# Weighing the attention's exponentials on ScalarE, and spreading a layer's modulations over nine groups of projections

## The chip, the cores and the metric

The kernel runs on one core of a Trainium2 chip. The metric is device time in microseconds (us), from one launch; the times here are medians of a few runs. The engines are TensorE (PE in the rows, with PEld for its weight loads), VectorE (DVE), ScalarE (ACT), GpSimd (POOL) and SyncE (SP), whose queue issues most loads by DMA.

## The reference, cut to what matters

An encoder trunk of two layers for 256 tokens of width 1024: layer 0 mixes tokens with RWKV-7, layer 1 with dilated attention, and behind each comes a mixture of experts (MoE). Every sub-layer is modulated: `shift`, `scale` and `gate` are rows of `silu(c) @ ada_w[layer] + ada_b[layer]`, six of width 1024 in each layer. The change lies in the attention, where each of 8 heads has three groups of keys, and the three results are merged by their softmax denominators:

```python
def _dilated_group(q, k, v, slopes, window, dilation):
    ...
    scores = jnp.where(valid, scores + alibi[None, None], NEG_INF)
    m = jnp.max(scores, axis=-1, keepdims=True)
    e = jnp.exp(scores - m)
    den = jnp.sum(e, axis=-1, keepdims=True)
    o = jnp.einsum('brhnqk,brhnkd->brhnqd', e, vblk) / den
    lse = (m + jnp.log(den))[..., 0]
    ...

def dilated_attention_mix(h, w_qkv, w_o):
    ...
    o = jnp.stack(outs)
    alpha = jax.nn.softmax(jnp.stack(lses), axis=0)
    merged = jnp.sum(alpha[..., None] * o, axis=0).reshape(bsz, s, d)
    return jnp.einsum('bsd,de->bse', merged.astype(h.dtype), w_o)
```

## The kernel before, in words

The attention is `heads()`. It takes the 8 heads as four pairs (`hp` 0 to 3). For each pair and each of three groups of keys (`g`), `project(hp, g)` makes q, k and v: a weight tile of 1 MB comes by SP's queue into `wring`, `weights()` splits it into two fp16 halves of which the sum is the weight (`wh` by ACT in L469 or L465/L466, `wl` by DVE in L473 or, for the second half of q's and v's weights, by POOL in L467), and PE multiplies the pieces in 48 matmuls of 128x256 (`qkv`, L271). The result is split in the same way (`qh` by ACT, `ql` by DVE).

`scores()` makes the scores of a group (`sc` on PE), adds the distance and takes the row maximum on DVE (L1800 to L1805), and ACT takes the exponential in place with the row sum (L1809). `merge()` is a chain of tiny DVE steps (L1816 to L1828) with one exponential on ACT (L1820); it gives `wg`, one factor per query, group and head. `values()` then multiplies each block of exponentials by its column of `wg` in place, in L1837: per head two blocks of 128x256 and four of 128x128. PE transposes the weighed blocks (`eT`, L275), ACT and DVE split the transposes (`eh`, `el`), PE multiplies them with v (`av`), and ACT and DVE split the result into `mh` and `ml`.

Beside this run two other jobs. The modulations of layer 1 are 32 *eighths*, four modulations by eight slices of 128 rows of `w_ada`. `ada()` takes an eighth from a ring of two buffers (`aring`, loaded by SP's queue), and DVE adds it, times `silu`, to `acc` in two pieces of 512 columns (L374 for the first eighth of a modulation, L376 for the others). After the last eighth of one, PE sums `acc` over the partitions (`ada` matmuls). For the gates (modulations 2 and 5) ACT's queue first loads the bias (L442) and DVE adds the two sums to it (L448). `ADA_PARTS` says how many eighths are handled behind each group of projections. The second job is the output weights: POOL multiplies them by gate 2 in L590, in four pieces per tile.

The program is written in the order of the loops in L1866 to L1894, and a scheduler puts each engine's instructions into a fixed order when the kernel is built. So the `merge` and `values` of a pair run while PE does the first projections of the next pair, and the engines wait for one another at run time. Pair 3 has no next pair; its cover is the output projection (`wo`). The MoE of layer 1 follows, whose 96 weight tiles of 1 MB come through the same SP queue.

Of the kernel before, what the change touches and what calls it, by code (L numbers as in the profile page):

```python
# [14 lines left out]
AF = mybir.ActivationFunctionType  # L15
ALU = mybir.AluOpType
# [16 lines left out]
RANK = dict(X=0, C=1, R=2, F=3, D=4, G=5, S=6, H=6, W=7, A=2.5)  # L33
OFFSET = dict(X=0, C=-6, R=-4, F=-2, D=-2, G=-1, S=0, H=0, W=0, A=8)

ADA_PARTS, PACE = (4, 4, 4, 4, 4, 4, 4, 4, 0), 4.0


C_TMG, C_CMG, C_ADAB, C_C, C_FG = 0, 16, 32, 128, 136
# [195 lines left out]
def trunk(ctx, tc, names, aps, out, stages=("rwkv", "moe0", "attn", "moe1"), dbg=None, ring=2):  # L235
# [12 lines left out]
    def bank(name="ps", tag="ps"):  # L248
        return psum[-1][tag].tile([128, 512], F32, name=name, tag=tag)
# [23 lines left out]
    def tr(o, i):  # L273
        pe_work[0] += 0.25
        return on_pe(nc.tensor.transpose(o, i, IDENT[0:i.shape[0], 0:i.shape[0]]))  # L275
# [27 lines left out]
    V, A, P = nc.vector, nc.scalar, nc.gpsimd  # L303
# [157 lines left out]
    def split(hi, lo, src, by, eng=None):  # L461

        if eng:
            if by != 1.0:
                A.activation(out=src, in_=src, func=AF.Copy, scale=by)  # L465
            A.activation(out=hi, in_=src, func=AF.Copy)  # L466
            eng.tensor_tensor(out=lo, in0=src, in1=hi, op=ALU.subtract)  # L467
            return
        A.activation(out=hi, in_=src, func=AF.Copy, scale=by)  # L469
        if by == 1.0:  # L470
            V.tensor_tensor(out=lo, in0=src, in1=hi, op=ALU.subtract)
            return
        V.scalar_tensor_tensor(out=lo, in0=src, scalar=by, in1=hi, op0=ALU.mult, op1=ALU.subtract)  # L473
# [1238 lines left out]
    def triple(o, lhs, rhs, start, stop):  # L1712

        for n, (a, b) in enumerate(((0, 0), (1, 0), (0, 1))):
            mm(o, lhs[a], rhs[b], start=start and n == 0, stop=stop and n == 2, skip_group_check=True)
# [6 lines left out]
    def heads(outer, mh, ml, before, c4):  # L1722
# [43 lines left out]
        scale = 128 ** -0.5  # L1766
# [64 lines left out]
        def values(hp, a, qkv, E, wg):  # L1831

            eh, el = (pool.tile([128, 8, 128], F16, name=n) for n in ("eh", "el"))
            for g in range(3):
                for t in range(NTT):
                    e = E[g][:, a, t * KW[g]:(t + 1) * KW[g]]
                    V.tensor_scalar(out=e, in0=e, scalar1=wg[:, t, g, a:a + 1], scalar2=None, op0=ALU.mult)  # L1837
            blocks = [E[0][:, a, t * 256 + kt * 128:t * 256 + kt * 128 + 128] for kt in range(2) for t in range(NTT)]
            blocks += [E[g][:, a, t * 128:(t + 1) * 128] for g in (1, 2) for t in range(NTT)]
            for n in range(2):  # L1840
                ps = bank(name="eT", tag="eT")
                for b in range(4):
                    tr(ps[:, b * 128:(b + 1) * 128], blocks[4 * n + b])
                split(*(v[:, 4 * n:4 * n + 4].rearrange("p b n -> p (b n)") for v in (eh, el)), ps, WSC)
            po = bank(name="av", tag="eT")
            vcol = slice(a * 128, a * 128 + 128)

            def av(o, v, c, start, stop):
                triple(o, [t[:, v[1], vcol] for t in qkv[v[0]][2]],
                       [t[:, c].rearrange("p b n -> p (b n)") for t in (eh, el)], start, stop)  # L1850

            for kt in range(2):
                av(po[:, 0:S], (0, kt), slice(2 * kt, 2 * kt + 2), kt == 0, False)
            for g in (1, 2):
                for t in range(NTT):
                    av(po[:, t * 128:(t + 1) * 128], (g, t), slice(2 + 2 * g + t, 3 + 2 * g + t), False,
                       g == 2 and t == 1)
            split(*(v[:, 2 * hp + a].rearrange("p (l r) -> p r l", r=NTT) for v in (mh, ml)),
                  po[:, 0:S].rearrange("p (r l) -> p r l", r=NTT), 1.0 / WSC)
# [6 lines left out]
        for hp in range(4):  # L1866
# [20 lines left out]
            wg = merge(st)  # L1887
# [211 lines left out]
```

## Time and profile before

| | us |
|---|---|
| median of 3 runs | 1186.47 |
| lowest, highest | 1184.41, 1190.94 |
| profiled execution, its own time | 1182.29 |
| its span, first to last instruction | 1180.5 |

| engine | busy us | share of the span |
|---|---|---|
| PE | 1040.8 | 88% |
| PEld | 682.5 | 58% |
| DVE | 616.8 | 52% |
| ACT | 432.4 | 37% |
| POOL | 148.7 | 13% |

The profile is of one execution. Busy time of PE is from modelled ends of pipelined matmuls. The granted clock is the share of TensorE's full clock that the chip allowed; over the span it was 0.943. A row of a timeline gives start, length, engine, line and operation; what stands in brackets at its end is the idle time of the engine before it and the instruction that ended that. "x8" means eight instructions in a row, merged into one row.

### The profile page before, as it was taken

What the parts mean: (1) busy time and instruction counts of PE and PEld (TensorE: products, weight loads), DVE (VectorE), ACT (ScalarE), POOL (GpSimd) and SP (SyncE); (2) the same over time, 40 slices, a digit from 0 to 9 for tenths busy, and PEclk for the clock granted to TensorE, in tenths of its full rate; (3) what the DMA queues carried; (4) which work ended last, traced back from release to release, by engine and by line L of the source; (5) the groups of instructions that cost most, each with busy time, mean ns of one, the idle gap of its engine ahead of it and who ended that gap; (6) DMA issues with size and microseconds to landing.
All of it is one profiled execution on the core that took longest, in us unless ns stands there. A gap on an engine that the chain in (4) does not pass through costs nothing.

```text
span 1180.5 us, 25023 instructions
## 1 busy us (share of the span) xinstructions
PE 1040.8 (88%) x10580; PEld 682.5 (58%) x10580; DVE 616.8 (52%) x1458; ACT 432.4 (37%) x915; POOL 148.7 (13%) x110
## 2 busy tenths in 40 slices
PE   7789999998978998978987799899979999789886
PEld 2576677766757655435442388777858754354422
DVE  4864678578485446213111467988885762131112
ACT  2634455455445342101000377555544621010012
POOL 1100010010012600000000112123373000000000
PEclk9879899899988899989999999998989999899999
DMA  9561524325233676998999987877744589989995
GB/s 366 207 220 60 180 67 159 114 89 167 73 130 132 263 286 250 400 414 361 422 421 421 420 346 262 310 268 284 255 173 150 212 352 395 416 362 421 420 421 238
DMA packets 53197, 322.01 MB, mean 273 GB/s; under 512 B 5922, under 2 KB 6562, under 8 KB 21458
## 3 DMA queue, kind: packets, MB, share of 16 engines
q1 hardware_dynamic: 51986, 315.88, 68.7%
q0 software_dynamic: 800, 3.36, 0.8%
q8 instruction: 87, 1.43, 0.5%
q10 hardware_dynamic: 288, 1.05, 0.3%
q14 instruction: 36, 0.29, 0.1%
HBM read 319.22 MB, written 1.05 MB: 271 GB/s over the span
## 4 chain that ended last, share of the span: by engine, by line
PE 23%; DMA 21%; DVE 8%; ACT 2%; issue 1%; ACTq 0%; SPq 0%; DVEq 0%
DMA wring<-in_w_moe_dram 21%; PE qkv L271 11%; PE gu L271 3%; DVE acc L376 2%; PE xT L271 1%; PE wo L271 1%; DVE wl L473 1%; PE acc L271 1%; PE dn L271 1%; PE av L271 1%; PE eT L275 1%; PE sc L271 1%; ACT sq L491 0%; DVE ql L473 0%; DVE E L1837 0%
## 5 line engine op out<-in xcount | busy, mean ns | idle before, releaser
L271 PE MATMUL gu<-wring,xT 128*32 128x512 f32 x1024 | 132.5, 617 | 18.0 <-DMA wring<-in_w_moe_dram 10.8
L376 DVE SCALAR_TENSOR_TENSOR acc<-aring,silu,acc 128x512 f32<-128x512 f32 x140 | 116.1, 859 | 13.2 <-DMA aring<-in_w_ada_dram 13.0
L467 POOL TENSOR_TENSOR wl<-wring,wh 128x1024 f16<-128x1024 f32 x24 | 57.7, 2406 | 409.4 <-DMA wring<-in_w_qkv_dram 248.3
L271 PE MATMUL qkv<-hl,wh 128*128 128x256 f16 x384 | 106.2, 277 | 2.0 <-DVE hl L1762 2.0
L271 PE MATMUL qkv<-hh,wh 128*128 128x256 f16 x384 | 106.3, 277 | 1.6 <-ACT hh L1761 1.6
L271 PE MATMUL qkv<-hh,wl 128*128 128x256 f16 x384 | 106.1, 277 | 1.2 <-DVE wl L473 1.1
L271 PEld LDWEIGHTS gu<-wring,xT 128*32 128x32 f32 x1024 | 31.3, 112 | 101.5 <-issue 78.1
L271 PEld LDWEIGHTS <-wh 128*128 128x128 f16 x768 | 76.3, 100 | 13.1 <-issue 3.6
L271 PE MATMUL dn<-wring,hidT 128*32 128x256 f32 x1024 | 66.2, 407 | 18.1 <-ACT hidT L1564 18.1
L473 DVE SCALAR_TENSOR_TENSOR wl<-wring,wh 128x1024 f16<-128x1024 f32 x56 | 70.6, 1266 | 16.6 <-ACT wh L469 16.6
L271 PE MATMUL acc<-y,back 128*128 128x512 f32 (+1 forms) x144 | 64.2, 568 | 10.3 <-DVE y L1591 8.1
L469 ACT ACTIVATE wh<-wring 128x1024 f16<-128x1024 f32 x56 | 58.6, 1050 | 35.6 <-PE qkv L271 30.9
L271 PEld LDWEIGHTS xT<-oh,x 128*128 128x128 f32 x512 | 59.0, 192 | 21.1 <-issue 9.2
L1366 DVE SCALAR_TENSOR_TENSOR sg<-sg,gu 128x256 f32<-128x256 f32 x16 | 6.7, 420 | 119.3 <-ACT sg L1365 119.3
L271 PE MATMUL xT<-oh,x 128*128 128x128 f32 x512 | 63.5, 280 | 2.5 <-DVE oh L1475 2.5
L1591 DVE TENSOR_TENSOR y<-dn,ga 128x512 f32<-128x512 f32 x28 | 19.4, 692 | 87.1 <-PE dn L271 55.5
L1365 ACT ACTIVATE sg<-gu 128x256 f32<-128x256 f32 x16 | 6.1, 384 | 147.3 <-PE gu L271 147.3
L271 PEld LDWEIGHTS dn<-wring,hidT 128*32 128x32 f32 x1024 | 32.3, 116 | 48.0 <-ACT hidT L1564 22.0
L271 PE MATMUL qkv<-wl,hh 128*128 128x256 f16 x192 | 54.0, 281 | 0.0
L271 PE MATMUL qkv<-wh,hh 128*128 128x256 f16 x192 | 53.9, 281 | 0.0
L271 PE MATMUL qkv<-wh,hl 128*128 128x256 f16 x192 | 53.9, 281 | 0.0
L1507 ACT ACTIVATE back<-bT 128x256 f32<-128x256 f32 x16 | 6.2, 386 | 129.7 <-PE acc L271 129.7
(355 smaller groups left out, 2096.5 us busy)
## 6 DMA issues: line engine op xcount, KB each, us to landing
wring<-in_w_moe_dram SPq DMA_DIRECT2D x192, 1024.0 KB, 19.8
aring<-in_w_ada_dram SPq DMA_DIRECT2D x96, 512.0 KB, 4.7
wring<-in_w_qkv_dram SPq DMA_DIRECT2D x36, 1024.0 KB, 8.7
wring<-in_w_kr_dram SPq DMA_DIRECT2D x8, 1024.0 KB, 5.4
wring<-in_w_vl_dram SPq DMA_DIRECT2D x8, 640.0 KB, 4.6
wring<-in_w_rwo_dram SPq DMA_DIRECT2D x4, 1024.0 KB, 8.2
wring<-in_w_ato_dram SPq DMA_DIRECT2D x4, 1024.0 KB, 6.9
x<-in_x_dram POOLq DMA_DIRECT2D x2, 512.0 KB, 7.7
```

The costliest lines, as they stand in the source:

```text
L271: return on_pe(nc.tensor.matmul(out=o, lhsT=lhsT, rhs=rhs, start=start, stop=stop, **kw))
L275: return on_pe(nc.tensor.transpose(o, i, IDENT[0:i.shape[0], 0:i.shape[0]]))
L376: V.scalar_tensor_tensor(out=acc[:, s], in0=w[:, s], scalar=silu[:, k:k + 1], in1=acc[:, s], op0=ALU.mult, op1=ALU.add)
L467: eng.tensor_tensor(out=lo, in0=src, in1=hi, op=ALU.subtract)
L469: A.activation(out=hi, in_=src, func=AF.Copy, scale=by)
L473: V.scalar_tensor_tensor(out=lo, in0=src, scalar=by, in1=hi, op0=ALU.mult, op1=ALU.subtract)
L1365: A.activation(out=o, in_=ps[:, 0:256], func=AF.Tanh, scale=0.5)
L1366: V.scalar_tensor_tensor(out=o, in0=o, scalar=1.0, in1=ps[:, 0:256], op0=ALU.add, op1=ALU.mult)
L1507: A.activation(out=back, in_=ps[:, 0:S], func=AF.Copy)
L1591: V.tensor_tensor(out=y, in0=py[c], in1=gates[i, 5][:, c * 512:(c + 1) * 512], op=ALU.mult)
```

## The change

The weighing of L1837 goes from VectorE to ScalarE, as a copy with a scale per partition: 48 instructions in all, six for each of eight heads. And the 32 eighths of layer 1's modulations are dealt out to nine groups of projections (five times four, then four times three) in place of eight groups of four. The numbers of `ADA_PARTS` go by `3 * hp + g`, so they cover pairs 0 to 2.

```diff
-ADA_PARTS, PACE = (4, 4, 4, 4, 4, 4, 4, 4, 0), 4.0
+ADA_PARTS, PACE = (4, 4, 4, 4, 4, 3, 3, 3, 3), 4.0
...
             for g in range(3):
                 for t in range(NTT):
                     e = E[g][:, a, t * KW[g]:(t + 1) * KW[g]]
-                    V.tensor_scalar(out=e, in0=e, scalar1=wg[:, t, g, a:a + 1], scalar2=None, op0=ALU.mult)
+                    A.activation(out=e, in_=e, func=AF.Copy, scale=wg[:, t, g, a:a + 1])
```

Three places show how the fixed order moves. The first is ACT at pair 0, from the split of q of the next pair on. `E0` to `E2` are the exponentials of the three groups, `eT` the transposes in PSUM, `eh` their fp16 heads, `wh` heads of projection weights. Before:

```order
L469 ACTIVATE qh01_9673<-qkv_9672 128x512
L469 ACTIVATE wh_9816<-wring_8799 128x1024
L469 ACTIVATE eh_9512<-eT_9520 128x512
L469 ACTIVATE eh_9512<-eT_9527 128x512
L469 ACTIVATE mh_8688<-av_9534 128x2x128
L469 ACTIVATE eh_9555<-eT_9563 128x512
L466 ACTIVATE wh_9820<-wring_8799 128x1024
L469 ACTIVATE eh_9555<-eT_9570 128x512
```

With the change:

```order
L469 ACTIVATE qh01_9673<-qkv_9672 128x512
L469 ACTIVATE wh_9816<-wring_8799 128x1024
L1837 ACTIVATE E0_9184<-E0_9184,wg_9497 128x256 x2
L1837 ACTIVATE E1_9425<-E1_9425,wg_9497 128x128 x2
L1837 ACTIVATE E2_9468<-E2_9468,wg_9497 128x128 x2
L469 ACTIVATE eh_9512<-eT_9520 128x512
L469 ACTIVATE eh_9512<-eT_9527 128x512
L1837 ACTIVATE E0_9184<-E0_9184,wg_9497 128x256 x2
L1837 ACTIVATE E1_9425<-E1_9425,wg_9497 128x128 x2
L1837 ACTIVATE E2_9468<-E2_9468,wg_9497 128x128 x2
L466 ACTIVATE wh_9820<-wring_8799 128x1024
```

The six weighings of the first head stand ahead of its splits, and the six of the second head behind them.

The second place is DVE in the merge of pair 1. `den`, `mm` and `wg` are the merge's small tiles, `acc` the accumulator of a modulation. Before:

```order
L376 SCALAR_TENSOR_TENSOR acc_10033<-aring_10274,silu_103,acc_10033 128x512 x2
L1822 TENSOR_TENSOR den_10325<-wg_10320,st0_10006 128x4
L1824 TENSOR_TENSOR mm_10317<-wg_10320,st1_10241 128x4
L1825 TENSOR_TENSOR den_10325<-den_10325,mm_10317 128x4
L374 TENSOR_SCALAR acc_10614<-aring_10278,silu_103 128x512
L1824 TENSOR_TENSOR mm_10317<-wg_10320,st2_10292 128x4
L374 TENSOR_SCALAR acc_10614<-aring_10278,silu_103 128x512
L1825 TENSOR_TENSOR den_10325<-den_10325,mm_10317 128x4
L367 TENSOR_TENSOR modc_107<-ada_10282,cols_66 128x8
L1826 RECIPROCAL den_10325<-den_10325 128x4
```

With the change:

```order
L1822 TENSOR_TENSOR den_10312<-wg_10307,st0_10006 128x4
L1824 TENSOR_TENSOR mm_10304<-wg_10307,st1_10241 128x4
L376 SCALAR_TENSOR_TENSOR acc_10033<-aring_10274,silu_103,acc_10033 128x512
L1825 TENSOR_TENSOR den_10312<-den_10312,mm_10304 128x4
L376 SCALAR_TENSOR_TENSOR acc_10033<-aring_10274,silu_103,acc_10033 128x512
L1824 TENSOR_TENSOR mm_10304<-wg_10307,st2_10279 128x4
L1825 TENSOR_TENSOR den_10312<-den_10312,mm_10304 128x4
L1826 RECIPROCAL den_10312<-den_10312 128x4
L1828 TENSOR_TENSOR wg_10307<-wg_10307,den_10312 128x2x2 x3
L473 SCALAR_TENSOR_TENSOR ql01_10484<-qkv_10482,qh01_10483 128x512
```

The two L374, which begin the next modulation, and the split `ql01` now stand behind the merge. On PE the first transposes of pair 1 follow 10 matmuls of the projection then running where 17 stood, and the matmuls of the finished modulation stand behind them. In pair 0 the first transposes follow 18 where 9 stood.

The third place is the merge of pair 2, on DVE and on POOL. `ga5` is gate 5 of the layer, `wl` the fp16 rests of projection weights. DVE before:

```order
L1819 TENSOR_TENSOR wg_11115<-st2_11087,mm_11112 128x2x2
L473 SCALAR_TENSOR_TENSOR wl_11293<-wring_10176,wh_11292 128x1024
L1822 TENSOR_TENSOR den_11120<-wg_11115,st0_10822 128x4
L1824 TENSOR_TENSOR mm_11112<-wg_11115,st1_11061 128x4
L1825 TENSOR_TENSOR den_11120<-den_11120,mm_11112 128x4
L1824 TENSOR_TENSOR mm_11112<-wg_11115,st2_11087 128x4
L1825 TENSOR_TENSOR den_11120<-den_11120,mm_11112 128x4
L473 SCALAR_TENSOR_TENSOR ql00_11235<-qkv_11233,qh00_11234 128x512
L1826 RECIPROCAL den_11120<-den_11120 128x4
```

DVE with the change:

```order
L1819 TENSOR_TENSOR wg_11115<-st2_11087,mm_11112 128x2x2
L448 TENSOR_TENSOR ga5_11078<-ga5_11078,ada_11080 128x512
L1822 TENSOR_TENSOR den_11120<-wg_11115,st0_10813 128x4
L1824 TENSOR_TENSOR mm_11112<-wg_11115,st1_11043 128x4
L1825 TENSOR_TENSOR den_11120<-den_11120,mm_11112 128x4
L473 SCALAR_TENSOR_TENSOR wl_11293<-wring_10176,wh_11292 128x1024
L448 TENSOR_TENSOR ga5_11078<-ga5_11078,ada_11083 128x512
L1824 TENSOR_TENSOR mm_11112<-wg_11115,st2_11087 128x4
L473 SCALAR_TENSOR_TENSOR ql00_11235<-qkv_11233,qh00_11234 128x512
L1825 TENSOR_TENSOR den_11120<-den_11120,mm_11112 128x4
L473 SCALAR_TENSOR_TENSOR wl_11352<-wring_10408,wh_11351 128x1024
L1826 RECIPROCAL den_11120<-den_11120 128x4
```

POOL before:

```order
L467 TENSOR_TENSOR wl_11229<-wring_10113,wh_11228 128x1024
L590 TENSOR_TENSOR wring_11220<-wring_11220,ga2_9226 128x512 x4
L590 TENSOR_TENSOR wring_11222<-wring_11222,ga2_9226 128x512 x4
L467 TENSOR_TENSOR wl_11356<-wring_10421,wh_11355 128x1024
L467 TENSOR_TENSOR wl_11420<-wring_10485,wh_11419 128x1024
```

POOL with the change:

```order
L467 TENSOR_TENSOR wl_11229<-wring_10113,wh_11228 128x1024
L467 TENSOR_TENSOR wl_11356<-wring_10408,wh_11355 128x1024
L590 TENSOR_TENSOR wring_11220<-wring_11220,ga2_9226 128x512 x4
L590 TENSOR_TENSOR wring_11222<-wring_11222,ga2_9226 128x512 x4
L467 TENSOR_TENSOR wl_11420<-wring_10472,wh_11419 128x1024
```

The two additions of gate 5 come into the merge of pair 2, and one split more; on POOL a split moves ahead of eight gatings. ACT issues the load of gate 5's bias behind the exponentials of `E1` of pair 2, where it issued it behind those of `E0`. PE does 20 more matmuls of projections, and the second one of gate 5, ahead of the first transposes of this pair. In pair 3, ACT splits two halves of output weights ahead of its first weighing, and four more output matmuls stand ahead of the first transposes, two more behind them.

## Rows read from the trace of the kernel before

**Rows 1.** The page, the chain that ended last: share of the span by engine.
```profile
PE 23%; DMA 21%; DVE 8%; ACT 2%; issue 1%; ACTq 0%; SPq 0%; DVEq 0%
```

**Rows 2.** The chain in order of time, its tail: start us, us, what.
```profile
1137.12 19.80 DMA wring<-in_w_moe_dram
```

**Rows 3.** Waits of SP's DMA queue, 860–960: us in total, times, longest.
```profile
SPq L153 <- DVE wl L473: 50.8, 10, 10.4
```

**Rows 4.** Stretches: us, busy PE, PEld, DVE, ACT, POOL, then PEclk, DMA, GB/s.
```profile
752.00:782.00 30.00, 25.63 (x208) 21.40 (x207) 24.44 (x32) 13.35 (x18) 6.58 (x3) 0.89 0.83 304
...
808.00:828.00 20.00, 17.57 (x136) 14.64 (x137) 16.61 (x38) 8.61 (x15) 5.80 (x2) 0.83 0.62 233
...
873.00:890.00 17.00, 9.23 (x77) 7.82 (x75) 15.05 (x32) 7.10 (x17) 10.24 (x6) 0.80 0.19 63
...
890.00:930.00 40.00, 40.00 (x377) 35.81 (x376) 20.32 (x25) 21.42 (x31) 8.51 (x4) 1.00 0.53 185
```

**Rows 5.** PE's waits in 678–950 us: us in total, times, longest.
```profile
PE eT L275 <- DVE E L1837: 11.2, 4, 7.8
PE ada L271 <- DVE acc L376: 4.4, 3, 2.6
```

**Rows 6.** One 2 us window of PE: us, busy, clock, DMA share, GB/s.
```profile
756.00:758.00 2.00, 2.00 (x12) 0.50 0.91 352
```

**Rows 7.** Groups by form, 678–950 us: busy us, mean ns, idle before.
```profile
L1837 DVE TENSOR_SCALAR E<-E,wg 128x128 f32<-128x128 f32 x32 | 8.9, 336 | 0.0
...
L1837 DVE TENSOR_SCALAR E<-E,wg 128x256 f32<-128x256 f32 x16 | 4.9, 345 | 0.0
...
L1809 ACT ACTIVATE E<-E,neg 128x256 f32<-128x256 f32 x16 | 7.9, 497 | 0.9 <-DVE neg L1805 0.9
```

**Rows 8.** Timeline of ACT, pairs 2 and 3: start, us, instruction.
```profile
869.42 0.38 ACT L1809 ACTIVATE E<-E,neg 128x128 f32<-128x128 f32 x1
869.71 0.19 ACT L1809 ACTIVATION_READ_ACCUMULATOR E<-E,neg 128x1 f32 x1
...
936.15 1.99 ACT L469 ACTIVATE wh<-wring 128x1024 f16<-128x1024 f32 x2
```

**Rows 9.** Timeline of DVE, pair 0 and the quarter behind it.
```profile
746.23 1.91 DVE L1837 TENSOR_SCALAR E<-E,wg 128x256 f32<-128x256 f32 x8
...
749.32 2.73 DVE L376 SCALAR_TENSOR_TENSOR acc<-aring,silu,acc 128x512 f32<-128x512 f32 x4
...
752.30 2.74 DVE L1837 TENSOR_SCALAR E<-E,wg 128x128 f32<-128x128 f32 x4
...
773.88 3.27 DVE L376 SCALAR_TENSOR_TENSOR acc<-aring,silu,acc 128x512 f32<-128x512 f32 x2
```

**Rows 10.** The page, the modulations' loads: KB each, us to landing.
```profile
aring<-in_w_ada_dram SPq DMA_DIRECT2D x96, 512.0 KB, 4.7
```

**Rows 11.** Timeline of DVE, then of PE, pair 1.
```profile
814.25 0.48 DVE L374 TENSOR_SCALAR acc<-aring,silu 128x512 f32<-128x512 f32 x1 [1.33 <-PE ada L271]
...
816.58 2.31 DVE L1837 TENSOR_SCALAR E<-E,wg 128x256 f32<-128x256 f32 x10
...
812.64 0.51 PE L271 MATMUL ada<-cst,acc 128*128 128x1 f32 x3 [0.91 <-DVE acc L376]
```

**Rows 12.** Timeline of PE, pair 2, group 1.
```profile
846.47 1.13 PE L271 MATMUL ada<-acc,cst 128*128 128x512 f32 x2 [0.85 <-DVE acc L376]
```

**Rows 13.** Timelines of DVE, PE and POOL, the merge of pair 2.
```profile
872.98 2.35 DVE L1819 TENSOR_TENSOR wg<-st,mm 128x4 f32<-128x4 f32 x3
...
881.59 0.47 PE L275 MATMUL eT<-cst,E 128*128 128x128 f32 x1 [7.77 <-DVE E L1837]
...
868.14 11.89 POOL L590 TENSOR_TENSOR wring<-wring,ga 128x512 f32<-128x512 f32 x8
```

**Rows 14.** Timeline of DVE, the merge of pair 3.
```profile
934.55 0.31 DVE L1819 TENSOR_TENSOR wg<-st,mm 128x4 f32<-128x4 f32 x3
```

**Rows 15.** The two loads of a gate's bias (L442), attention layer.
```profile
DMA to landing us min/median/max: 3.7/4.1/4.5
```

## The prediction, made before the change was run

> **What bounds the kernel now.** I read four views, in this order. The chain that ended last, by engine, gives TensorE (PE) 23% of the span, weight loads by DMA 21% and VectorE (DVE) 8% [rows 1]. The same chain in order of time ends in MoE weights that land one 19.8 us load after the other [rows 2], so the last stretch belongs to DMA. The attention, from about 678 to 950 us, comes ahead of it and is a PE stretch with holes. If it ends earlier, does the kernel? The queue that issues the loads waited 50.8 us between 860 and 960 us for DVE to have read weight buffers [rows 3], and DMA was only 0.53 busy in 890–930 us [rows 4]. So the loads follow the attention, and I pass on what is gained there one for one.
>
> The third view is what PE waited for inside the attention: 11.2 us in four waits of the transposes eT for the weighing in L1837, one of them 7.8 us, and 4.4 us in three waits of modulation matmuls for the accumulation in L376 [rows 5]. The fourth is the table of stretches: PE is granted 0.89, 0.83 and 0.80 of its clock in 752–782, 808–828 and 873–890 us [rows 4]. That is 30 x 0.11 + 20 x 0.17 + 17 x 0.20 = 10 us of work not done at full speed, and it follows the holes: 756–758 us, right behind the weighing waits, ran at 0.50, the 1.2 GHz level [rows 6]. A part of the slow time lies in the holes themselves, where it costs nothing (in 873–890 PE is busy 9.23 of 17 us), so I count 8. About 16 us of waits and 8 us behind them are what can be had at most.
>
> **The weighing itself.** 48 instructions leave DVE: 32 of 128x128 and 16 of 128x256, 8.9 + 4.9 = 13.8 us of DVE [rows 7]. ScalarE (ACT) has no such instruction in the trace, but it has exponentials of the same two shapes: 0.38 us for 128x128, with the next instruction starting 0.29 us on [rows 8], and 0.497 us for 128x256 [rows 7], of which I let it start the next after 0.4. A head is two of the larger and four of the smaller: 2 x 0.4 + 4 x 0.29 = 2.0 us back to back, against 13.8 / 8 = 1.7 on an undisturbed DVE. The bounds are 1.7 (as on DVE) and 2.6 (whole durations end to end); I take 2.0, the nearest rows being the same shape on the same engine. So a head is not weighed faster. What counts is when it starts, and what DVE does meanwhile.
>
> **Pair 0 (745–757 us).** DVE weighs head 0 and two pieces of head 1 in 1.91 us, then splits, then adds four halves of modulation weights (2.73 us), and only at 752.30 weighs the other four pieces, in 2.74 us, 0.69 each where 0.34 is usual [rows 7, 9]. Pair 0 has 11.2 - 7.8 = 3.4 us of PE's weighing waits, and of the 3.3 us of half clock in 752–782 I give it 2. On ACT the second head's pieces follow the first head's with two splits between, so they are weighed near 751.5, and nothing is left to wait for there. The first transposes' wait, about half of the 3.4, falls by 1.0 us, since 18 matmuls stand ahead of them where 9 stood, at 40.00 / 377 = 0.106 us each [rows 4], and grows by 0.15, the longer first weighing: some 0.8 stays, and I keep 0.6 of half clock. Gain 5.4 - 1.4 = **4.0** (2 to 5).
>
> **The modulation wait of pair 0.** The longest of the three L376 waits is 2.6 us [rows 5], behind two halves that took 3.27 us [rows 9]. The quarter itself is unmoved. PE comes 4 us earlier, but the ring of these weights has two buffers and a load lands 4.7 us after issue [rows 10], so it can't come forward as much. **-0.5** (-1 to +2).
>
> **Pair 1 (809–828 us).** Two L374 stood between the small steps of the merge, and the first waited 1.33 us for PE to read the accumulator [rows 11]. In the new order they and a split ql01 stand behind the merge, so its weights are ready 1.33 + 2 x 0.45 + 0.9 (a split of 0.68 and a short wait, taken together) = 3.1 us earlier than 816.6, at 813.5, and the first piece is weighed at 813.9. PE's modulation wait of 0.91 us goes. But the matmuls of modulations that PE did before the transposes go behind them, and seven fewer of the projection stand ahead (10 for 17): it comes to its transposes at 812.64 - 0.91 = 811.7, and finds a new wait of 2 us. Of the 20 x 0.17 = 3.4 us at half clock, something may go. Gain **1.8** (0 to 3.5).
>
> **Pair 2, groups 0 to 2.** Gate 5 moves from group 1 to group 2. The wait of 0.85 us at 846.47 goes, and its two matmuls (1.13 us) [rows 12] move into the hole that follows. Together **2.0** (0.5 to 2.5).
>
> **Pair 2, the merge (872–890 us).** This is the largest hole, 7.77 us before 881.59 [rows 13]. Three tiny subtractions take 2.35 us beside POOL's eight gatings (868.14 to 880), where they take 0.31 elsewhere [rows 13, 14]. In POOL's new order the split wl_11356 stands ahead of these eight, and it waits for ACT, so the eight move out of the merge: some 6 us of slowed steps go. In exchange two additions of gate 5 (L448) and a third split (wl_11352) come into DVE's queue among the steps of the merge. The first L448 needs the bias that ACT loads behind the exponentials of E1, which end at 869.8 [rows 8]; such a load lands after 4.1 us [rows 15], at about 874. Behind it stand, with 0.68 us for 512 columns (2.73 / 4 [rows 9]): two L448 and ql at 0.68 each, two wl of 1024 columns at 1.36, and seven small steps at 0.2: 6.2 us, weights ready at 880.1 in place of 881.2. First transposes at about 880.8. Meanwhile PE has 20 more matmuls to do ahead of them, 2.1 us at 0.106 each, and gate 5's, counted above. Gain 0.8 + 2.1 = 2.9, taken as **3.0**; 1 if the clock stays low longer, 7 if the bias is no obstacle.
>
> The rule in the way: DVE's steps here have both inputs in SBUF, and three of them stretched from 0.31 to 2.35 us beside POOL [rows 13, 14]. The Trainium skill, SBUF — State Buffer, section Who interferes with whom, says that a DVE instruction with two SBUF inputs contends with a GpSimd instruction that reads SBUF, and that the later of two that want the shared ports blocks for the whole of the other. By that, the moved split wl_11356 would hold up wl_11352 and the steps around it in pair 2, and the sum would be 1 to 2 us smaller; the row agrees with the rule, but no row shows which of the two would come first.
>
> **Pair 3.** ACT's new order has two splits of 1 us each (1.99 us for two [rows 8]) ahead of the weighing, which DVE did at once; some six more output matmuls, put ahead of the pair's `av`, cover the larger part of that. **-0.5** (-2 to +1).
>
> **Sum.** 4.0 - 0.5 + 1.8 + 2.0 + 3.0 - 0.5 = 9.8 us. The profiled execution took 1182.29 us (span 1180.5), 4.2 below the median of the runs shown, 1186.47. So 1172.5 on its basis, and **1176.7** as a median.
>
> **Rivals.**
> *All holes close.* Three quarters of the 24 us go, 18: the clock is 1.00 in 890–930 [rows 4], where nothing is waited for, which speaks for it; the waits I find anew at pairs 0, 1 and 2 speak against. 1168.5. Chance 0.12.
>
> *The waits change hands.* The holes remain and only their releaser's name changes: the bias load before L448, the ring of modulation weights that is now drawn on up to the last group of pair 2, ACT's queue in place of DVE's. Or the loads of the MoE don't come earlier, because another reader of the buffers than DVE holds them. DVE's 15.05 busy of 17 us in 873–890 [rows 4] shows how many of the steps there stay. Gain 2 to 3: 1184. Chance 0.21.
>
> *Slower: ACT's order in time.* ACT takes its instructions in order. In pair 0 the six weighings of head 1 stand ahead of the splits wh, mh and eh, and those of head 0 ahead of its own eh. If in each head the splits that PE waits for come 1.0 us later (half of the 2.0) without cover, that is 8 x 1.0 = 8 us, with no gain elsewhere but what I gave for the gate (2) and about as much again of half clock behind the new holes: 1186.5 + 8 = 1194.5. It decides where fewer than 2.0 us of other matmuls lie between a head's last transpose and its av matmuls. For it: ACT takes 0.38 and 0.497 us where DVE took 0.336 and 0.345 [rows 7, 8]. Against it: DVE has 24.44 busy of 30 us in 752–782, ACT 13.35 [rows 4]. The Trainium skill, Perfetto Trace Analysis, section Optimizing Scalar/DVE Operations, puts it as a choice: an operation that has a fast mode on DVE is faster there, and moving some to Scalar may make sense if DVE is saturated; the rows bear out both halves, the first over a whole instruction, the second only in these stretches. Chance 0.09.
>
> That the change doesn't do what it says can be left out: the 48 weighings stand on ACT in the new order.
>
> **How the numbers follow.** Forecast 0.58, all holes 0.12, change of hands 0.21, slower 0.09. The ends of my terms add to more than they will together; taking half of each spread, the forecast's own range is 1171 to 1182. With most of the first rival and of the second the range is 1167.5 to 1186.5. A measurement of this kernel tells about 0.5%, 5.9 us, from no change: faster means below 1180.5. Faster: 0.58 x 0.90 + 0.12 + 0.21 x 0.15 = 0.67. Slower: 0.09, with 0.01 from the second rival 0.10. The rest, 0.23, is within 0.5%.
>
> **What would show it.** Right: no eT wait on DVE is left, those on ACT add to some 6 us; 752–782 us at a clock of 0.95 or more; the subtractions of pair 2's merge at about 0.3 us; PE's wait at pair 2 between 2 and 5 us, with an L448 that waited for the bias. Wrong: waits of av or eT on ACT's eh of over 1 us in most heads (the slower rival), DVE as full as before in 873–890 with a wait of 7 us again (change of hands), or the attention ended 10 us earlier and the last MoE load not (the one-for-one step).

## The result, and the profile after

The changed kernel took 1177.55 us in the median of 6 runs (1173.87 to 1179.24), the kernel before 1185.74 (6 runs, 1183.01 to 1190.94). The ratio is 0.993, with a 95% interval of 0.990 to 0.996; a second set of runs gave 0.9947 (0.993 to 0.997). So it is faster by 6 to 8 us, where 9.8 were forecast.

The two profiles differ by less than the medians: 1178.76 us (span 1177.0) after, 1182.29 (span 1180.5) before. The profiled execution before was 3.5 us below its kernel's median, the one after 1.2 above. Which parts of a difference belong to the change and which to the single execution is therefore asked of all the profiles below, not of two.

The page of the changed kernel, busy time of each engine:

```profile
PE 1035.3 (88%) x10580; PEld 678.3 (58%) x10580; DVE 602.8 (51%) x1410; ACT 447.2 (38%) x963; POOL 148.1 (13%) x110
```

ACT has taken 15 us and DVE given 14. The chain in order of time, its tail:

```profile
1133.53 19.87 DMA wring<-in_w_moe_dram
```

The last MoE load began 3.6 us earlier than in [rows 2], and the span is 3.5 shorter: the end moved with the attention. The busy time by stretch has the columns of [rows 4]:

```profile
752.00:782.00 30.00, 26.02 (x233) 22.65 (x230) 23.97 (x29) 15.14 (x20) 6.64 (x3) 0.94 0.89 336
...
808.00:828.00 20.00, 17.50 (x168) 15.28 (x167) 13.31 (x27) 14.92 (x28) 2.48 (x2) 1.00 0.68 247
...
846.00:873.00 27.00, 20.60 (x176) 16.95 (x175) 22.89 (x31) 13.21 (x36) 19.14 (x10) 0.94 0.53 190
...
873.00:890.00 17.00, 13.79 (x125) 11.26 (x125) 10.59 (x21) 11.53 (x24) 10.67 (x8) 1.00 0.38 134
```

The clock in 752–782, 808–828 and 873–890 us is 0.94, 1.00 and 1.00 where it was 0.89, 0.83 and 0.80 [rows 4], and in 873–890 us PE is busy 13.79 us, not 9.23. (A second profile of the changed kernel, `again` below, has 0.89, 0.91 and 0.90 in the same windows, so a part of this is the single execution.) But 846–873 has got worse: 20.60 us busy of 27 at a clock of 0.94. The kernel before, the same window:

```profile
846.00:873.00 27.00, 25.99 (x232) 21.90 (x233) 20.43 (x31) 13.49 (x28) 21.63 (x14) 1.00 0.61 217
```

What PE waited for in 678–950 us after the change, with the columns of [rows 5]:

```profile
PE qkv L271 <- DVE wl L473: 8.6, 6, 2.7
PE eT L275 <- ACT E L1837: 3.2, 3, 2.1
PE ada L271 <- DVE acc L376: 2.6, 1, 2.6
PE qkv L271 <- DVE hl L1762: 2.0, 1, 2.0
PE eT L275 <- DVE ml L473: 2.0, 3, 1.4
PE ada L271 <- DVE ga L448: 1.9, 1, 1.9
```

The 11.2 us of waits for the weighing on DVE are 3.2 on ACT now. Beside them stand waits that are new or longer: 1.9 us for gate 5, 2.0 for `ml`, and 8.6 for `wl`, for which PE waited 1.1 us in the kernel before.

To compare runs I cut the attention where PE starts the score matmuls, which come in two groups for each pair: I from the second scores of pair 0 to the first of pair 1 (holds pair 0's values), II to the first of pair 2 (pair 1's values), III to the second of pair 2, IV to the first of pair 3 (pair 2's merge and values), V to the first router matmul. In us, from the timeline of PE in each profile:

| kernel | I | II | III | IV | V | sum |
|---|---|---|---|---|---|---|
| before | 51.46 | 63.69 | 20.60 | 47.27 | 39.39 | 222.4 |
| changed | 48.53 | 60.51 | 26.93 | 43.14 | 39.61 | 218.7 |
| again (the changed kernel) | 49.43 | 63.58 | 21.83 | 45.34 | 39.59 | 219.8 |
| act_only | 48.32 | 63.29 | 21.04 | 49.48 | 39.58 | 221.7 |
| parts_only | 51.20 | 60.91 | 25.91 | 50.12 | 39.39 | 227.5 |
| bias_early | 49.59 | 61.03 | 23.64 | 48.29 | 39.59 | 222.1 |
| gate_late | 49.48 | 65.16 | 22.30 | 49.22 | 39.60 | 225.8 |
| gate_late_dve | 53.52 | 66.33 | 21.62 | 46.07 | 39.38 | 226.9 |
| both_nogate | 48.32 | 60.72 | 22.35 | 41.24 | 39.58 | 212.2 |
| act_nogate | 49.24 | 60.25 | 21.21 | 40.62 | 39.59 | 210.9 |
| gate_spread | 49.52 | 62.10 | 20.91 | 40.14 | 39.62 | 212.3 |
| both_spread | 50.58 | 61.79 | 22.52 | 44.63 | 39.59 | 219.1 |
| all_spread | 48.40 | 63.25 | 21.21 | 39.32 | 39.83 | 212.0 |
| dve_spread | 51.15 | 65.54 | 20.17 | 42.05 | 39.40 | 218.3 |

One profile is one draw: kernels with the same order in I to III differ there by some 6 us in sum. Means over equal orders are used where there are several.

The five stretches together, from the second scores of pair 0 to the first router matmul, with the columns of [rows 4]. Before, after, and `again`:

```profile
729.00:951.41 222.41, 203.78 (x1750) 168.63 (x1747) 177.06 (x316) 119.99 (x217) 66.78 (x34) 0.95 0.67 244
```

```profile
728.82:947.54 218.72, 199.24 (x1750) 164.68 (x1747) 164.93 (x268) 134.37 (x265) 65.78 (x34) 0.98 0.69 253
```

```profile
727.20:946.97 219.77, 202.05 (x1751) 167.06 (x1749) 167.78 (x268) 134.65 (x265) 61.69 (x34) 0.97 0.69 252
```

The length less PE's busy time is what PE stood idle: 18.6 us before, 19.5 and 17.7 after. So in these profiles PE's waits changed places and hardly shrank in sum. What got shorter is its busy time, by 4.5 and 1.7 us for the same matmuls, at a granted clock of 0.98 and 0.97 in place of 0.95.

### The profile page after: what moved, and what is told of

Same layout as the page of the kernel before. It is cut to its first block, busy times and chain, and to the rows that moved or that the text cites. A ratio compares the mean times of both kernels' runs of the same rounds, so it can differ in the third digit from the quotient of the medians.

```text
span 1177.0 us, 25033 instructions
## 1 busy us (share of the span) xinstructions
PE 1035.3 (88%) x10580; PEld 678.3 (58%) x10580; DVE 602.8 (51%) x1410; ACT 447.2 (38%) x963; POOL 148.1 (13%) x110
## 5 line engine op out<-in xcount | busy, mean ns | idle before, releaser
L376 DVE SCALAR_TENSOR_TENSOR acc<-aring,silu,acc 128x512 f32<-128x512 f32 x140 | 120.8, 889 | 14.2 <-DMA aring<-in_w_ada_dram 14.1
L467 POOL TENSOR_TENSOR wl<-wring,wh 128x1024 f16<-128x1024 f32 x24 | 55.2, 2303 | 402.1 <-DMA wring<-in_w_qkv_dram 245.4
L271 PEld LDWEIGHTS xT<-oh,x 128*128 128x128 f32 x512 | 59.0, 192 | 21.1 <-issue 9.2
```

Of the source, the lines that this page charges most:

```text
L271: return on_pe(nc.tensor.matmul(out=o, lhsT=lhsT, rhs=rhs, start=start, stop=stop, **kw))
L376: V.scalar_tensor_tensor(out=acc[:, s], in0=w[:, s], scalar=silu[:, k:k + 1], in1=acc[:, s], op0=ALU.mult, op1=ALU.add)
```

## The experiments

### The changed kernel again, and its two parts

`again` is the changed kernel. `act_only` takes back the dealing, `parts_only` the engine:

```diff
 act_only
-ADA_PARTS, PACE = (4, 4, 4, 4, 4, 3, 3, 3, 3), 4.0
+ADA_PARTS, PACE = (4, 4, 4, 4, 4, 4, 4, 4, 0), 4.0
 parts_only
-                    A.activation(out=e, in_=e, func=AF.Copy, scale=wg[:, t, g, a:a + 1])
+                    V.tensor_scalar(out=e, in0=e, scalar1=wg[:, t, g, a:a + 1], scalar2=None, op0=ALU.mult)
```

> The changed kernel once more, for a second profile. In the first one the attention was 6.3 us ahead of the kernel before at the start of pair 2's projections, and had lost all of it 21 us later, in four waits of projections for wl (L473): 1.15, 2.73, 2.31 and 1.36 us. Theory A (the fixed order puts halves of modulation additions ahead of the weight splits on VectorE, beside POOL's gatings): the waits for wl between 835 and 865 us are there again, 5 to 9 us together. Theory B (an accident of one execution, such as a load that came late): under 2 us together, and the attention ends 8 us earlier than in the kernel before. Ratio 0.993 in either case, between 0.990 and 0.996.

> The weighing on ScalarE alone, with the eighths as in the kernel before (eight groups of four). If the terms stand by themselves: pair 0 gains its 3 us (the same order on PE as in the change), pair 1 and the groups of pair 2 nothing (waits of 0.9, 0.85 and 0.5 us stay), the hole ahead of pair 2's transposes stays at 7 to 8 us because POOL's eight gatings stay beside the merge. About 3 to 4 us under the kernel before, ratio 0.997. If the weighing were the whole of it: ratio 0.993 and a hole of under 4 us at pair 2. If ScalarE's order cost what the slower rival said: ratio 1.003 or more.

> The eighths over nine groups alone, with the weighing on VectorE. If the terms stand by themselves: pair 0 is as before (weighing waits of 3.4 us, half clock behind them), pair 1 gains 2 to 3 us, pair 2's groups lose 4 to 7 us in waits for wl as in the change, the merge of pair 2 gains about 4. Together 0 to 3 us under the kernel before, ratio 0.998 to 1.000. If the dealing of the eighths were the whole of it: ratio 0.993.

Measured: 0.9947 (0.993 to 0.997), 0.9966 (0.9945 to 0.9987) and 1.0029 (1.0008 to 1.0051). The waits for splits came again in `again`, 4.6 us between 836 and 868 (3.3 for DVE's, 1.3 for POOL's): fewer than 5, but no accident. The weighing alone brings half to two thirds of the gain, the dealing alone loses. By product the two would be at 0.9995, together they are at 0.993 and 0.9947. The place where they need each other is IV: 49.48 and 50.12 us alone, 43.14 and 45.34 together, although with the new dealing IV also holds the four matmuls of gate 5, about 2.1 us of PE, that stand in III with the old one. In `act_only` the hole is as before, beside the same slow subtractions as [rows 13]. First PE, then DVE:

```profile
880.70 0.47 PE L275 MATMUL eT<-cst,E 128*128 128x128 f32 x1 [7.85 <-ACT E L1837]
```

```profile
871.90 2.34 DVE L1819 TENSOR_TENSOR wg<-st,mm 128x4 f32<-128x4 f32 x3
```

In `parts_only` the gatings have left the merge and stand beside the weighing. The timeline of DVE, of POOL and of PE:

```profile
880.30 9.91 DVE L1837 TENSOR_SCALAR E<-E,wg 128x256 f32<-128x256 f32 x8
```

```profile
880.45 2.18 POOL L467 TENSOR_TENSOR wl<-wring,wh 128x1024 f16<-128x1024 f32 x1 [11.78 <-ACT wh L466]
882.59 9.97 POOL L590 TENSOR_TENSOR wring<-wring,ga 128x512 f32<-128x512 f32 x8
```

```profile
882.83 0.55 PE L275 MATMUL eT<-cst,E 128*128 128x128 f32 x3 [1.58 <-DVE E L1837]
...
887.70 0.48 PE L275 MATMUL eT<-cst,E 128*128 128x128 f32 x1 [0.75 <-DVE E L1837]
```

Eight weighings take 9.91 us, 1.24 each on average, and PE waits for one after another of them. In the changed kernel the same stretch of POOL runs beside ACT:

```profile
879.33 2.13 POOL L467 TENSOR_TENSOR wl<-wring,wh 128x1024 f16<-128x1024 f32 x1 [11.28 <-ACT wh L466]
881.42 10.86 POOL L590 TENSOR_TENSOR wring<-wring,ga 128x512 f32<-128x512 f32 x8
```

```profile
879.29 2.08 ACT L1837 ACTIVATE E<-E,wg 128x256 f32<-128x256 f32 x6
...
882.32 2.08 ACT L1837 ACTIVATE E<-E,wg 128x256 f32<-128x256 f32 x6
```

There six take 2.08 us, as in pair 0, where POOL is idle:

```profile
746.10 2.08 ACT L1837 ACTIVATE E<-E,wg 128x256 f32<-128x256 f32 x6 [0.72 <-DVE wg L1828]
748.09 1.14 ACT L469 ACTIVATE eh<-eT 128x512 f16<-128x512 f32 x2
749.13 2.07 ACT L1837 ACTIVATE E<-E,wg 128x256 f32<-128x256 f32 x6
```

So the dealing moved POOL's gatings from the merge onto the weighing, and the weighing had just gone to an engine that they don't slow.

### Gate 5's bias earlier

The bias is loaded when gate 5's first eighth is taken; the rest of `ada()` is as it was.

```diff
...
+        if (i, m, k) == (1, 5, 0):
+            bias_load(i, m)
...
```

> The changed kernel with gate 5's bias loaded when its first eighth is taken in place of its last. The prediction had the first L448 wait for that load; in the first profile PE then waited 1.9 us for L448 at 875.0. If that wait is worth its length: 1.9 us under the changed kernel, ratio about 0.991. If the merge behind it is bound by other steps of VectorE, the wait only moves to the transposes: ratio 0.993. The scheduler also puts 20 matmuls fewer ahead of the transposes here (18 of the second projection in place of 38), which could cost up to 2 us: ratio 0.995.

Measured: 0.9994 (0.997 to 1.002), slower than any of the three values expected. The wait for L448 went, but the scheduler then put POOL's order back: the eight gatings stand beside the merge again (lines are 7 higher here), and PE's hole with them. POOL, then PE:

```profile
866.23 11.89 POOL L597 TENSOR_TENSOR wring<-wring,ga 128x512 f32<-128x512 f32 x8
```

```profile
880.04 0.47 PE L275 MATMUL eT<-cst,E 128*128 128x128 f32 x1 [6.45 <-ACT E L1844]
```

It is a miss as a test of the wait. As a test of the gatings it points the same way as `act_only`, with the new dealing in place, though PE's order changed too, as the expectation says.

### The gatings moved by hand

`gate_late` is `act_only` with the last two tiles' gatings behind POOL's split of pair 3, group 0's v (`tc.issue_after`, which only orders one engine); `gate_late_dve` does the same to the kernel before. `act_nogate` and `both_nogate` leave gatings out: the last two tiles' of `act_only`, the first two tiles' of the changed kernel. The order of all other instructions is that of the kernel they come from.

```diff
-            w = weights(pool, gated(stream.take(("ato", u)), gates[1, 2], 2).rearrange("p (k n) -> p k n", k=2), 2)
+            with tc.issue_after(pool_split[0].ins) if u >= 2 else nullcontext():
+                wk = gated(stream.take(("ato", u)), gates[1, 2], 2)
+            w = weights(pool, wk.rearrange("p (k n) -> p k n", k=2), 2)
...
```

> The weighing on ScalarE, the eighths dealt as in the kernel before, and POOL's last eight gatings put behind the second half's split of the weights of v of pair 3, group 0 (their place in the changed kernel). PE's order is that of the run with the weighing alone, where the hole ahead of pair 2's transposes was 7.85 us and the three subtractions of the merge took 2.34 us. Theory A (the hole is made by POOL's gatings beside the merge, and the dealing of the eighths helped only by moving them): the three subtractions take about 0.3 us, the hole is 1 to 3 us, from the second score group of pair 2 to the first of pair 3 it takes 43 to 45 us in place of 49.5, ratio 0.990 to 0.993. Theory B (the dealing helps by what it takes out of VectorE's queue): the hole stays at 6 us or more, ratio 0.996 to 0.998.

> The kernel before, with POOL's last eight gatings moved as in gate_late, and the weighing left on VectorE. Theory A: the gatings now stand beside the weighing of pair 2, and its instructions take about 1.2 us each in place of 0.34, as they did with the eighths alone dealt anew (9.91 us for eight); the stretch from the second score group of pair 2 to the first of pair 3 takes 47 to 51 us, no better than the 47.3 of the kernel before. Rival: the weighing has one input of this kind only and takes 0.34 us; 42 to 45 us.

> The weighing on ScalarE, the eighths as in the kernel before, and the gating of the last two tiles left out (eight instructions of L590; the order of all the rest is the same). Theory A: nothing of POOL is left beside the merge of pair 2; the hole of 7.85 us falls to 1 to 3 us, as in gate_late, so that the gatings cost nothing where gate_late puts them: the two stretches to the first scores of pair 3 agree within 1 us. If gate_late's new place costs something in its turn, this one is 2 us or more shorter.

> The changed kernel without the gating of the first two tiles of output weights (eight instructions of L590 left out; the order of all the rest is the same). In its two profiles PE waited 7.6 and 5.0 us for wl between 838 and 868 us, where L376 took up to 2.1 us each and wl up to 2.5. Theory A (the waits are made by these gatings stretching the additions that stand ahead of wl): L376 and wl take 0.74 and 1.2 us, the waits for wl there come to under 2.5 us, and from the first score group of pair 2 to the second it takes 20 to 22 us in place of 26.9 and 21.8. Theory B (VectorE's order or late loads alone make them): 4 us or more of such waits stay.

`gate_late` came to 0.998 (0.996 to 1.000): by the time, theory B; by the rows, theory A and a new wait. The timeline of DVE, POOL and PE (L1827 and L594 are L1819 and L590 here):

```profile
873.56 0.31 DVE L1827 TENSOR_TENSOR wg<-st,mm 128x4 f32<-128x4 f32 x3
...
885.50 10.58 POOL L594 TENSOR_TENSOR wring<-wring,ga 128x512 f32<-128x512 f32 x7
...
877.87 0.33 PE L275 MATMUL eT<-cst,E 128*128 128x128 f32 x1 [1.88 <-ACT E L1845]
...
900.42 0.40 PE L271 MATMUL qkv<-hh,wl 128*128 128x256 f16 x1 [5.90 <-POOL wl L469]
```

The subtractions take 0.31 us and the hole is 1.88, as foretold. But the eight in a row hold POOL until 896, and PE waits 5.9 us for the next split on it. In the changed kernel the row of eight ended at 892.3, and nothing waited. `gate_late_dve` shows half of what was expected: eight weighings at 0.24 us, done before the gatings, and four at 0.96 on average beside POOL (L1845 is L1837):

```profile
877.22 1.92 DVE L1845 TENSOR_SCALAR E<-E,wg 128x256 f32<-128x256 f32 x8
...
880.30 3.82 DVE L1845 TENSOR_SCALAR E<-E,wg 128x128 f32<-128x128 f32 x4
```

IV took 46.07 there, between what theory A and its rival expected, and no gain to speak of. In `act_nogate` the hole fell to 1.88 us, as foretold, and it gives the price: IV is 40.62 us without those gatings, 8.9 less than in `act_only` with all else in the same order. (The times of these three, 1182.6 us for `gate_late_dve`, 1174.3 for `act_nogate` and 1176.86 for `both_nogate`, are single runs.)

`both_nogate` went against theory A. The waits for `wl` between 836 and 868 stay:

```profile
PE qkv L271 <- DVE wl L473: 4.8, 3, 2.3
```

III took 22.35 us, just above the 20 to 22 that A expected, but that decides nothing, since `again` has 21.83 with the gatings in place. So the gatings lengthen the waits at most. Whether the new order or late loads make them, no run parts. ACT's next instruction there is the split of a tile that has not landed, and the split of q and the `wh` that PE needs stand behind it. ACT in `both_nogate`, then in the changed kernel, and PE in the latter:

```profile
843.02 1.06 ACT L465 ACTIVATE wring<-wring 128x1024 f32<-128x1024 f32 x1 [5.13 <-DMA wring<-in_w_qkv_dram]
```

```profile
842.90 1.06 ACT L465 ACTIVATE wring<-wring 128x1024 f32<-128x1024 f32 x1 [6.51 <-DMA wring<-in_w_qkv_dram]
```

```profile
848.74 0.28 PE L271 MATMUL qkv<-hh,wl 128*128 128x256 f16 x1 [2.73 <-DVE wl L473]
```

### A version that beats both

The gatings of the last two tiles in fours, in gaps of two projections: behind POOL's splits for group 1's q and group 2's q of pair 3. `gate_spread` does it to `act_only`, `both_spread` to the change, `dve_spread` to the kernel before; `all_spread` is `gate_spread` with all four tiles' gatings in pair 3, behind the splits for group 0's v, group 1's q, and group 2's q and v.

```diff
+            place = {2: (3, 1, 0), 3: (3, 2, 0)}.get(u)
+            with tc.issue_after(behind[place].ins) if place else nullcontext():
...
```

> As gate_late (weighing on ScalarE, eighths as in the kernel before), but POOL's last eight gatings in two fours: behind the split for group 1's q and behind the one for group 2's q of pair 3. Only POOL's order differs from the run with the weighing alone. In gate_late the hole at pair 2 fell to 1.88 us, but the eight in a row then held the next split on POOL, and PE waited 5.9 us for that. Theory: with fours in gaps of two projections nothing waits for POOL, and the stretch from the second score group of pair 2 to the first of pair 3 takes 40.5 to 42 us, as without these gatings (40.62); from the first projections' scores of pair 0 to the end of the attention 211 to 216 us; ratio 0.986 to 0.991. Rival: the fours beside VectorE's splits in pair 3 stretch these, PE waits there for wl, and pair 3 gives back 3 us or more: ratio 0.993 to 0.997.

> The changed kernel with the last eight gatings in the two places of gate_spread; only POOL's order differs from the change. In the change these eight stand beside the splits behind pair 2's merge, which takes 43.1 to 45.3 us from the second score group of pair 2 to the first of pair 3. Without anything of POOL there: 41 to 42. If the dealing of the eighths is worth something by itself, this run is faster than gate_spread; if it only moved the gatings, as the stretches so far say (pair 1 gains 2.7 us, pair 2's groups lose as much), the two are within 0.2% of each other, both at 0.986 to 0.991.

> As gate_spread, but all four tiles' gatings are in pair 3: behind POOL's splits for group 0's v, group 1's q, group 2's q and group 2's v. The first eight then leave pair 2's groups 1 and 2, where they stretched VectorE's additions and splits. Theory: that stretch takes 20 to 21 us and loses its waits for wl, 1 to 2 us under gate_spread, ratio 0.985 to 0.990. Rival: four gatings (6 us) do not fit between two splits that are one projection (5.1 us) apart, PE waits for POOL, and it is 1 to 3 us slower than gate_spread.

> The kernel before with the last eight gatings in the two places of gate_spread, weighing on VectorE; only POOL's order differs from the kernel before. With nothing of POOL beside merge and weighing of pair 2 neither is stretched, so that the hole of 7.8 us falls to 1 to 3 us: ratio 0.991 to 0.995. The move of the weighing is then worth only what it gives at pair 0, about 3 us: gate_spread 0.002 to 0.003 below this one. Rival (the weighing on ScalarE is needed for the gain at pair 2): 47 us again for that stretch, ratio 0.998 or more.

Measured: `gate_spread` 0.987 (0.9846 to 0.9894), `both_spread` 0.9896 (0.9863 to 0.9928), `all_spread` 0.9851 (0.9819 to 0.9882), `dve_spread` 0.9914 (0.9891 to 0.9938). POOL and PE in `gate_spread` (L593 is L590):

```profile
889.06 6.92 POOL L593 TENSOR_TENSOR wring<-wring,ga 128x512 f32<-128x512 f32 x4
...
904.77 5.94 POOL L593 TENSOR_TENSOR wring<-wring,ga 128x512 f32<-128x512 f32 x4
...
874.58 0.33 PE L275 MATMUL eT<-cst,E 128*128 128x128 f32 x1 [1.69 <-ACT E L1844]
```

No wait for POOL is left, and IV takes 40.14 us, as without the gatings. From the first cut to the last PE stands idle for 11.4 us, against 18.6 before: here the waits themselves are gone. In `dve_spread` the hole is 1.81 us and IV 42.05, so the gain at pair 2 doesn't need the weighing on ACT. `both_spread` has 44.63 in IV where 41 to 42 were expected; the account of pair 2's merge below says why. `all_spread`, by stretch:

```profile
846.00:873.00 27.00, 25.64 (x231) 21.61 (x230) 18.51 (x41) 17.48 (x44) 4.25 (x2) 1.00 0.67 242
873.00:890.00 17.00, 16.57 (x162) 14.67 (x160) 9.41 (x11) 10.84 (x19) 13.01 (x8) 1.00 0.30 97
```

PE is busy 16.57 of 17 us in 873–890, where it was 9.23 [rows 4]. It is the fastest median, 1169.44 us beside 1186.06 of the kernel before on the same chip, though its interval and that of `gate_spread` overlap: that the last step is worth 2 us is not shown, and III, where its gain was expected, is no shorter (21.21 and 20.91). Both are faster than the change, from whose interval (0.990 to 0.996) theirs are apart. With the gatings out of the way the weighing on ACT is worth 0.9914 - 0.987 = 0.0044, some 5 us where I expected 3, but the two intervals overlap by a hair, so its size is rough; the dealing is worth nothing that can be seen (0.9896 with it, 0.987 without, the intervals overlapping).

## Why the prediction was right, step by step

**The weighing's price.** Forecast 2.0 us for a head, from the exponentials; measured 2.08 (the rows of pair 0 above), with these durations by form (busy us, mean ns, idle before):

```profile
L1837 ACT ACTIVATE E<-E,wg 128x128 f32<-128x128 f32 x32 | 10.2, 391 | 0.0
...
L1837 ACT ACTIVATE E<-E,wg 128x256 f32<-128x256 f32 x16 | 7.2, 500 | 2.8 <-DVE wg L1828 2.7
```

The price on DVE was misread. The last four weighings of pair 0, 0.69 us each by [rows 9], were three of 0.27 and one of 2.15 (least, middle and longest in ns):

```profile
L1837 DVE TENSOR_SCALAR E<-E,wg x4: 272/274/2153, 752.3 to 754.8; 128x128 f32<-128x128 f32 x4
```

The long one ran from 752.49 to 754.64, beside a split of POOL's from 752.44 to 754.56. So this row held the same kind of cost as the hole at pair 2, for an instruction with one tensor as input, and the forecast's 1.7 us for an undisturbed head contains it. By the eight in 1.91 us of [rows 9] a head took 1.4.

**Pair 0.** Forecast 4.0 - 0.5 = 3.5. The mean of I is 51.8 in the four kernels that weigh on DVE and 49.1 in the ten that weigh on ACT: 2.7. The first transposes wait 0.9 (0.8 forecast), the modulation wait of 2.6 stayed to the hundredth, and a part of the half clock stayed (0.94; 0.89 in `again`), below the 0.95 that was named as a sign. What the step had wrong is that nothing would be left to wait for at the second head. Its transposes now wait for `ml`, which stands on DVE behind a `wl` of 2.27 us, beside POOL's split, and two additions:

```profile
757.27 0.63 PE L275 MATMUL eT<-cst,E 128*128 128x128 f32 x4 [1.37 <-DVE ml L473]
```

All ten kernels that weigh on ACT show this wait, at 1.35 to 1.37 us.

**Pair 1, and groups 0 to 2 of pair 2.** This is the step that failed. I gave the dealing 1.8 + 2.0 = 3.8 us there. PE did find its new 2.1 us wait at pair 1, and II is 2.3 us shorter with the new dealing (61.4 on average over six kernels, 63.7 over eight with the old one). But III is 2.7 longer (23.9 and 21.1), although the four matmuls of gate 5, some 2.2 us of PE, have left it for IV. Among the ten kernels that weigh on ACT alone, II is 1.3 shorter and III 2.1 longer. In III PE stands idle for 4.1 to 7.6 us in the six profiles with the new dealing and for 1.2 to 3.1 in the eight with the old one; with the new one most of it is for `wl`, which stands behind modulation additions in DVE's queue. PE also comes 4 to 6 us earlier in the two profiles of the change, and ACT meets a tile that has not landed; but `parts_only` has 25.91 in III with 0.63 us of that wait on ACT, and `act_only` 21.04 with 2.45, so the late tile alone doesn't make it. So the dealing gave about - 0.4 (- 0.8 among those ten) where + 3.8 was forecast. Groups of equal order say the same more roughly: I to III take 138.0 us on average with DVE and the old dealing (before, gate_late_dve, dve_spread: 135.75, 141.47, 136.86), 133.2 with ACT and the old one (act_only, gate_late, act_nogate, gate_spread: 132.65, 136.94, 130.70, 132.53), 135.2 with ACT and the new one (changed, again, both_spread: 135.97, 134.84, 134.89). By these the dealing costs 2.0, and the weighing gives 4.8 in place of 3.5. The spread within a group is larger than the 2.0, so whether the dealing costs anything is open; a gain of 3.8 it is not. Two things were in reach of the step: the six half additions that DVE now has in III, where it had two and the two of gate 5, were not costed, and a late load was considered for the modulations' ring and not for the projections' weights.

**The merge of pair 2.** Forecast 3.0 (1 to 7), from 47.27: measured 4.1 and 1.9. DVE's steps are the ones foretold: subtractions at 0.31 in place of 2.35, then a first L448 that waits for the bias, and the splits behind it. PE's wait of 2 to 5 us for the weighing is not there in this profile (0.2); it waits 1.9 for gate 5 instead, whose matmul stands ahead of the transposes.

```profile
870.44 0.31 DVE L1819 TENSOR_TENSOR wg<-st,mm 128x4 f32<-128x4 f32 x3
874.27 0.69 DVE L448 TENSOR_TENSOR ga<-ga,ada 128x512 f32<-128x512 f32 x1 [3.52 <-DMA ga<-in_p_adab_dram]
...
875.22 1.22 DVE L473 SCALAR_TENSOR_TENSOR wl<-wring,wh 128x1024 f16<-128x1024 f32 x1
876.35 0.68 DVE L448 TENSOR_TENSOR ga<-ga,ada 128x512 f32<-128x512 f32 x1
...
877.69 1.22 DVE L473 SCALAR_TENSOR_TENSOR wl<-wring,wh 128x1024 f16<-128x1024 f32 x1
```

The bias landed after 6.0 us here, and DVE waited 3.52; in `again` it landed after at most 3.8, and DVE waited 0.21. What the prediction missed is the other half of the bargain, that gatings which leave the merge come to stand beside the weighing, so that this term exists only because both edits were made.

As for the rule of the shared ports, which would have taken 1 to 2 us from this term: in the first profile the merge ended at 879.34, just as POOL's moved split began (879.33), and it cost nothing. In `again`, where the bias came early and POOL's split began ahead of the merge's last three steps, these took 3.10 us in place of 0.31, and PE waited 2.60. POOL, DVE and PE:

```profile
875.02 2.22 POOL L467 TENSOR_TENSOR wl<-wring,wh 128x1024 f16<-128x1024 f32 x1 [7.45 <-ACT wh L466]
...
875.39 3.10 DVE L1828 TENSOR_TENSOR wg<-wg,den 128x4 f32<-128x4 f32 x3
...
877.92 0.33 PE L275 MATMUL eT<-cst,E 128*128 128x128 f32 x1 [2.60 <-ACT E L1837]
```

IV is 2.2 us longer there than in the first profile. `both_spread` repeats it, with 2.02 us for the three steps and the same wait of 2.60, and holds gate 5's matmuls besides; together they account for most of its 44.63 in IV. So the prediction left out of its sum a cost that came in one of the two profiles of the change. The contention also holds where it was not looked for, at the weighing. The Trainium skill, SBUF — State Buffer, section Who interferes with whom, names `tensor_scalar` among the instructions that can enter a two-port mode and so contend with GpSimd, and says that ACT never waits on anyone; 1.24 us for a weighing on DVE and 2.08 for six on ACT, both beside POOL, agree with it, though no run shows in which mode DVE worked.

**Pair 3.** Forecast - 0.5, measured - 0.2 (V). **The end, one for one.** From the first router matmul to the end it took 229.1 us before and 229.5 after; over all profiles it is 227.6 to 233.4, with no clear trend against the attention's length.

**The sum.** 9.8 forecast. By the means above, 138.0 - 135.2 = 2.8 in I to III, about 3.0 in IV and - 0.2 in V make 5.6; the runs say 6.3 and 8.2. The forecast lies close, but in part by luck: the dealing was off by about - 4 to - 6 us, while the weighing gave more than its 3.5 by these means. And most of the 9.8 was counted as waits that go, while in the profiles of the change PE's waits hardly shrank in sum (18.6, then 19.5 and 17.7) and the clock gave more than the waits.

**The rivals.** All holes closing needed the gatings out of the way, and `gate_spread` shows a good part of it (14 us). Waits that change hands are what happened in III, and over the attention as a whole, if not with that rival's time of 1184. Of the signs, the subtractions and the L448 that waits came as named; eT waits on DVE were to be gone, and 2.0 us are left, for `ml`; those on ACT were to be some 6 us, and are 3.2. The slower rival did not show: the weighing in ACT's queue costs PE 3.2 us in three waits, and no `av` waits on ACT for more than 0.4.

## What to carry to other kernels

When small instructions take many times their usual length, find out what runs beside them and move that, by an order on its own engine: here that alone brought the kernel before 10 us (`dve_spread`), with the weighing on ACT 14 (`gate_spread`), and 17 with all four tiles moved (`all_spread`); the change under study brought 6 to 8. A second edit can be worth something only with the first: measure both alone before either is credited. And a sum made against one profiled execution inherits its luck, here 3.5 us of 1186: read stretches from several.

## What the runs showed of the hardware

A VectorE instruction with one tensor and a column of scalars as inputs, fp32, 128x128 and 128x256 mixed, took 0.24 us alone (eight in 1.92, `gate_late_dve`) and 1.24 us beside POOL's split and gatings (eight in 9.91, `parts_only`); I had counted on that only for instructions with two tensors. One of 128x128 took 2.15 us beside one split of 2.12 in the kernel before. On ScalarE the same multiplication took 0.35 us of queue time (2.08 / 6) whether POOL worked or not (pairs 2 and 0 of the changed kernel).
